# Branch products ahead of the last gate columns, and those gate columns as seven half-size products

## The chip, the cores and the metric

The kernel runs on one core of one Trainium2 chip. The metric is the device time of one execution in microseconds (us). The kernel before takes 646.97 us, the median of 3 runs (646.88 to 647.17). The profiled execution, from which all durations here come, took 647.0 us; its span, from the first to the last instruction of the core, is 645.3 us.

## The reference

One decoder layer on 512 tokens of 1024 channels, all in float32. Only what the change touches is shown in full; the rest is told by its names.

```python
proj = x @ W_in                 # 1024 -> 512 q | 512 k | 512 v | 512 pool_in | 2048 gate logits
y_attn = moba_attention(q, k, v, rel_bias) @ w_branch_attn     # 8 heads x 64, then 512 -> 1024
y_pool = multiscale_pool(p, w_group, scale) @ w_branch_pool    # windows 2, 4, 8, 16, then 512 -> 1024
gates = sigmoid(g).reshape(B, S, 2, 1024)
mixed = gates[:, :, 0] * y_attn + gates[:, :, 1] * y_pool
h = layer_norm(ALPHA * x + mixed @ w_out)
a, u = split(h @ w_ffn_in, 2)                                  # 1024 -> 2 x 2816
a = causal_dwconv(a, conv_w, conv_b)
h = layer_norm(ALPHA * h + (gelu(a) * u) @ w_ffn_out)          # 2816 -> 1024
```

The 2048 gate columns are 16 tiles of 128 columns. Tile f (0 to 7) of the first half gates channels 128 f to 128 f + 127 of the attention branch, tile 8 + f the same channels of the pool branch. The two together are called gate pair f.

## The kernel before

**Numbers.** Every float32 operand is kept as two float32r tiles, `hi` (a rounded copy) and `lo` (the rest). The helper `split` makes them: a copy on ScalarE (line 69) and a subtraction on VectorE (line 70). The helper `mm3` (lines 190 to 192) makes one product as three matmuls: hi times hi, hi times lo, lo times hi. All matmuls take a 128 x 128 tile of weights as the stationary operand, and 512 tokens (or 256) as the moving one.

**Weights.** All weight tiles of the kernel stand in one list, `chunks`, in the order of use. `fetch` loads the next one from memory by the SP queue (line 117) into one of 3 raw buffers and splits it into one of 5 pairs of buffers (`RING`). `weights(i)` fetches up to 3 chunks (`LEAD`) ahead of the one that is used.

**Stages.** In order of the program:
1. The input projection and the attention. `order` lists the 28 tiles of the projection: q, k and pool inputs first, then the 16 gate tiles. Each, `in_tile`, is 8 x 3 matmuls of 512 tokens. `bg` puts the first tiles between the steps of the attention as work for TensorE; the last 9 tiles, all gates, come after the attention. Gate logits are copied to the 12 slots of `gates`; the last four tiles (`NLATE`) go through the sigmoid into `late`.
2. The split of the two branch inputs: `zT` (pool) and `oT` (attention), 4 tiles each.
3. Eight branch tiles, f = 0 to 7. Each is 4 x 3 matmuls of 512 tokens for the pool branch and as many for the attention branch. VectorE multiplies each result with its gate (line 485), GpSimd adds the two (line 488), and the sum is split into `mx_hi`, `mx_lo`. Both lie where `xT_hi` and `xT_lo` lay before.
4. The output projection (`wo`), the residual and the first LayerNorm. GpSimd's queue loads the residual `xs` (line 496) and the LayerNorm rows `lnb` (lines 500, 501) into the place that `gates` held.
5. The channel mixer. Its 22 pairs of columns (a and u) of 128 are computed, for pairs 4 to 17 (`SEVEN`), with seven products in place of eight.
6. The down projection, also with seven products, and the second LayerNorm.

**Seven products.** In `seven(f)` (line 697) a pair is a 2 x 2 block product: the 1024 input channels are cut in two halves, the two column tiles are the two blocks of the output's channels, and the 512 tokens are cut in two. A full pair would be 8 block products; a scheme with sums and differences of blocks needs 7, each of 4 x 3 matmuls of 256 tokens. The sums of weights are formed by loading: the raw tile X is loaded by SP (line 140) and another block is added to it by an accumulating load of GpSimd's queue (line 141); Y is formed from X and A on VectorE (line 152). So a pair has four chunks, A, X, D and Y. The differences of the activations are formed once by `t_form` (line 669) on VectorE, and split: nT1, T3, nT2, T4. Partial results are copied out of PSUM by ScalarE (lines 703, 708, 710) and added by VectorE (lines 712, 714, 715). The last product of a pair waits in `pending` and is issued inside the next pair.

**What sets the order.** A planner orders the instructions of each engine by a simulated timeline; the order in the program is the priority. Work that is ready can so be placed far ahead of its place in the program. The functions:

Of the kernel before, what the change touches and what calls it, by code (L numbers as in the profile page):

```python
# [36 lines left out]
NLATE = 4  # L37
KH = NF // 2
TAIL = 8
SEVEN = tuple(range(4, 18))  # L40
# [5 lines left out]
def layer_kernel(ctx: ExitStack, tc: tile.TileContext, xT, x, w_v, w_c, rel_bias, invcnt, w_group,  # L46
# [27 lines left out]
    spare = [("p", 2), ("p", 3)] + [("g", 8 * g + f) for f in range(KT) for g in range(2)]  # L74
# [8 lines left out]
    BR0 = len(chunks)  # L83
    chunks += [w_br[f] for f in range(KT)]
# [3 lines left out]
    fi_at = {}  # L88
    for f in range(NF):
        for q in "AXDY" if f in SEVEN else "au":  # L90
            fi_at[f, q] = len(chunks)
            chunks.append((f, q) if f in SEVEN else w_fi[2 * f + "au".index(q)])
# [5 lines left out]
    def fetch(pool=None, early=None):  # L98
        i = state["next"]
        state["next"] = i + 1  # L100
        for q, ahead in AHEAD.items():
            while coming[q] and (xu or q == "A") and fi_at[coming[q][0], q] <= i + (ahead if xu else 0):
                fetch_raw(coming[q].pop(0), q)
# [21 lines left out]
    coming = {q: list(SEVEN) for q in "DAX"}  # L125
    xu = None

    def fetch_raw(f, q):
        a, u = w_fi[2 * f], w_fi[2 * f + 1]
        if q == "A":  # L130
            r = wp.tile([P, D], F32, tag="wraw", name=f"araw{f}", bufs=3)
            nc.sync.dma_start(r, a)
        elif q == "D":
            r = xu.tile([P, S], F32, tag="draw", name=f"draw{f}", bufs=2)
            nc.sync.dma_start(r, u[:, S:])
        else:
            r = xu.tile([P, D], F32, tag="xraw", name=f"xraw{f}", bufs=2)
# [6 lines left out]
        raws[f, q] = r  # L144

    def fetch_seven(i, f, q):
        n = S if q == "D" else D
        raw = raws[f, "A" if q == "Y" else q]
        if q == "Y":

            for c, o in ((slice(0, S), raws[f, "X"][:, S:]), (slice(S, D), raw[:, :S])):
                nc.vector.tensor_tensor(raw[:, c], o, raw[:, c], op=ALU.add)
# [35 lines left out]
    def mm3(out_, w, a, start, stop, **kw):  # L188
        (wh, wl), (ah, al) = w, a
        nc.tensor.matmul(out_, wh, ah, start=start, stop=False, **kw)  # L190
# [3 lines left out]
    def split3(v, a):  # L194
        return tuple(t.rearrange("p (a c) -> p a c", a=a) for t in v)

# [150 lines left out]
    def in_tile(n):  # L347
# [11 lines left out]
        elif len(gslot) < NKEEP:  # L359
            gslot[j] = gates[:, len(gslot), :]  # L360
            nc.vector.tensor_copy(gslot[j], b)
        else:
            gslot[j] = late[:, len(gslot) - NKEEP, :]
            nc.scalar.activation(gslot[j], b, AF.Sigmoid)
# [66 lines left out]
    def bg(n=1):  # L431
        for _ in range(n):
            if len(todo) > NLATE:
# [23 lines left out]
    late = bp.tile([P, NLATE, S], F32, name="late")  # L457
# [6 lines left out]
    for k in range(4):  # L464
        split(oT_hi[:, k, :], oT_lo[:, k, :], oT[:, k, :])
    while todo:
        in_tile(todo.pop(0))
    mx_hi = act.tile([P, KT, S], F32R, tag="actT_hi", name="mx_hi")
    mx_lo = act.tile([P, KT, S], F32R, tag="actT_lo", name="mx_lo")
    ext = actp.enter_context(tc.tile_pool(name="ext", bufs=1, side="right"))  # L470
    for f in range(KT):
        if f == KT - LEAD:
            state["limit"] = WO0 + RING - 1
        wh, wl = split3(weights(BR0 + f), KT)
        for g in range(2):
            if gslot[8 * g + f].tensor is gates.tensor:
                nc.scalar.activation(gslot[8 * g + f], gslot[8 * g + f], AF.Sigmoid)
        m = []
        for br in (1, 0):
            b = bank(f"br{f}_{br}")  # L480
            for k in range(4):
                src = (zT_hi[:, k, :], zT_lo[:, k, :]) if br else (oT_hi[:, k, :], oT_lo[:, k, :])
                mm3(b, (wh[:, 4 * br + k, :], wl[:, 4 * br + k, :]), src, k == 0, k == 3)
            t = bp.tile([P, S], F32, tag="m", name=f"m{f}_{br}", bufs=4)
            nc.vector.tensor_tensor(t, gslot[8 * br + f], b, op=ALU.mult)
            m.append(t)
# [198 lines left out]
    for n in ("nT1", "T3", "nT2", "T4"):  # L685
        t_form(n)
# [250 lines left out]
```

## Time and profile before

| what | value |
|---|---|
| median of 3 runs | 646.97 us |
| profiled execution: time, span | 647.0 us, 645.3 us |
| TensorE busy (PE) | 634.8 us, 98% of the span |
| weight loads (PEld) | 551.2 us, 85% |
| VectorE (DVE) | 449.4 us, 70% |
| ScalarE (ACT) | 328.7 us, 51% |
| GpSimd (POOL) | 110.9 us, 17% |
| granted TensorE clock, mean | 0.997 |

The profile page gives the busy time of each engine, the span in 40 slices, the chain of work that ended last, and groups of instructions by line. A row of the timeline reads: start in us, duration in us, engine, line of the kernel, operation, output and inputs by the program's names with their shapes, count, and in brackets how long the engine was idle before and what ended that. Matmuls are pipelined, so the step from one matmul's start to the next is their cost, not the duration of the row. A row of the table by stretches reads: the stretch, its length, then for PE, PEld, DVE, ACT and POOL the busy us (and the count), the granted clock, the busy share of the DMA engines, and GB/s.

### The profile page before, as it was taken

To read this page: it belongs to the slowest core of one execution; us is meant where nothing else is said; L and a number is where in the kernel's file an instruction comes from. 1 tells how busy PE (TensorE), PEld (TensorE's weight loads), DVE (VectorE), ACT (ScalarE), POOL (GpSimd) and SP (SyncE) were. 2 spreads that over 40 slices of the span, in tenths; PEclk is the share of its full clock that TensorE was granted. 3 is DMA by queue.
4 is the path that set the end of the run, shared out by engine and by line. 5 is a ranking of instruction groups with operands and counts; after the bars stand their busy time and mean duration, and the time that the engine had idled before them with its cause. 6 is when DMAs were issued, how large, how long until landed. Compare 5 with 4: busy or idle time off the path is not lost.

```text
span 645.3 us, 9324 instructions
## 1 busy us (share of the span) xinstructions
PE 634.8 (98%) x3586; PEld 551.2 (85%) x3586; DVE 449.4 (70%) x666; ACT 328.7 (51%) x475; POOL 110.9 (17%) x153
## 2 busy tenths in 40 slices
PE   8999999999999999999999999999999999999994
PEld 6888787878788888888998999999998888888884
DVE  6456665564632476489686789888889649698696
ACT  6546556675522233206464555656557337455452
POOL 1605270311000123300010101011101101123202
PEclk9999999999999999999999999999999999999998
DMA  9643222213223236504067576877827964989905
GB/s 318 214 143 113 80 83 82 67 66 99 67 98 99 98 99 245 179 0 137 28 208 168 164 180 163 192 197 184 180 81 276 274 186 102 208 191 194 279 5 130
DMA packets 32540, 94.79 MB, mean 147 GB/s; under 512 B 3688, under 2 KB 3944, under 8 KB 32240
## 3 DMA queue, kind: packets, MB, share of 16 engines
q1 hardware_dynamic: 22832, 66.91, 31.1%
q0 software_dynamic: 9088, 26.24, 20.7%
q10 hardware_dynamic: 576, 1.05, 0.4%
q8 instruction: 28, 0.46, 0.3%
q14 instruction: 16, 0.13, 0.1%
HBM read 91.02 MB, written 3.17 MB: 146 GB/s over the span
## 4 chain that ended last, share of the span: by engine, by line
PE 94%; DVE 2%; POOL 2%; ACT 1%; DMA 0%; issue 0%; DVEq 0%; ACTq 0%; POOLq 0%
PE fi L190 5%; PE fi L192 5%; PE fi L191 5%; PE g L190 5%; PE g L191 5%; PE g L192 5%; PE sa L190 4%; PE sa L192 4%; PE sa L191 4%; PE v L291 3%; PE wo L192 2%; PE br L192 2%; PE br L190 2%; PE wo L190 2%; PE wo L191 2%; PE br L191 2%
## 5 line engine op out<-in xcount | busy, mean ns | idle before, releaser
L70 DVE TENSOR_TENSOR wlo<-wraw,whi 128x1024 fp32r<-128x1024 f32 (+1 forms) x77 | 100.4, 1308 | 50.8 <-ACT whi L69 49.8
L69 ACT ACTIVATE whi<-wraw 128x1024 fp32r<-128x1024 f32 (+1 forms) x76 | 78.8, 1040 | 97.9 <-PE g L191 23.6
L191 PE MATMUL fi<-hT_lo,whi 128*128 128x512 f32 (+1 forms) x168 | 56.7, 339 | 0.0
L192 PE MATMUL fi<-hT_hi,wlo 128*128 128x512 f32 (+1 forms) x168 | 56.7, 339 | 0.0
L190 PE MATMUL fi<-hT_hi,whi 128*128 128x512 f32 (+1 forms) x168 | 56.4, 340 | 0.0
L190 PE MATMUL g<-xT_hi,whi 128*128 128x512 f32 x128 | 50.3, 393 | 0.0
L192 PE MATMUL g<-xT_hi,wlo 128*128 128x512 f32 x128 | 49.9, 390 | 0.0
L191 PE MATMUL g<-xT_lo,whi 128*128 128x512 f32 x128 | 49.8, 389 | 0.0
L141 POOL DMA_DIRECT2D xraw<-in_w_fi x14 | 17.0, 1211 | 180.8 <-DVE y L631 69.0
L69 ACT ACTIVATE whi<-tw 128x1024 fp32r<-128x1024 f32 (+1 forms) x30 | 29.4, 984 | 25.1 <-PE fi L191 12.4
L70 DVE TENSOR_TENSOR wlo<-tw,whi 128x1024 fp32r<-128x1024 f32 (+1 forms) x30 | 33.3, 1126 | 9.3 <-ACT whi L69 9.2
L70 DVE TENSOR_TENSOR wlo<-araw,whi 128x1024 fp32r<-128x1024 f32 x28 | 33.9, 1221 | 6.0 <-ACT whi L69 5.7
L69 ACT ACTIVATE whi<-araw 128x1024 fp32r<-128x1024 f32 x28 | 29.4, 1061 | 13.3 <-PE sa L191 6.1
L192 PEld LDWEIGHTS fi<-hT_hi,wlo 128*128 128x128 f32 x168 | 31.9, 190 | 3.5
L191 PEld LDWEIGHTS fi<-hT_lo,whi 128*128 128x128 f32 x168 | 31.9, 190 | 3.4
L190 PEld LDWEIGHTS fi<-hT_hi,whi 128*128 128x128 f32 x168 | 31.6, 190 | 3.4
L191 PE MATMUL sa<-hT_lo,whi 128*128 128x256 f32 x112 | 31.6, 282 | 0.0
L190 PE MATMUL sa<-hT_hi,whi 128*128 128x256 f32 x112 | 31.6, 282 | 0.0
L192 PE MATMUL sa<-hT_hi,wlo 128*128 128x256 f32 x112 | 31.5, 282 | 0.0
L190 PE MATMUL sb<-T_hi,whi 128*128 128x256 f32 x112 | 31.3, 280 | 0.0
L190 PE MATMUL sa<-nT_hi,whi 128*128 128x256 f32 x112 | 31.3, 279 | 0.0
L192 PE MATMUL sa<-nT_hi,wlo 128*128 128x256 f32 x112 | 31.3, 279 | 0.0
(254 smaller groups left out, 1844.7 us busy)
## 6 DMA issues: line engine op xcount, KB each, us to landing
wraw<-in_w_c SPq DMA_DIRECT2D x28, 512.0 KB, 3.4
tw<-in_w_fo POOLq DMA_DIRECT2D x20, 512.0 KB, 8.3
wraw<-in_w_fi SPq DMA_DIRECT2D x16, 512.0 KB, 3.8
araw<-in_w_fi SPq DMA_DIRECT2D x14, 512.0 KB, 4.6
xraw<-in_w_fi SPq DMA_DIRECT2D x14, 512.0 KB, 4.3
xraw<-in_w_fi POOLq DMA_DIRECT2D x14, 512.0 KB, 6.6
tw<-in_w_fo SPq DMA_DIRECT2D x10, 512.0 KB, 5.8
wraw<-in_w_fo SPq DMA_DIRECT2D x10, 512.0 KB, 6.7
```

The source lines that it names most:

```text
L69: nc.scalar.activation(hi, src, AF.Copy)
L70: nc.vector.tensor_tensor(lo, src, hi.bitcast(F32), op=ALU.subtract)
L141: nc.gpsimd.dma_start(v, bass.AP(tensor=a.tensor, offset=a.offset, ap=[[pst, pn], [u.offset + S - a.offset, 2], [est, S]]), accum_op=ALU.add)
L190: nc.tensor.matmul(out_, wh, ah, start=start, stop=False, **kw)
L191: nc.tensor.matmul(out_, wh, al, start=False, stop=False, **kw)
L192: nc.tensor.matmul(out_, wl, ah, start=False, stop=stop, **kw)
L291: nc.tensor.matmul(bs[j], xs_[j][a], (wh, wl)[b], start=kt == 0 and n == 0, stop=False)
```

## The change

Gate pairs 0 to 3 are computed as before. Gate pairs 4 to 7 become seven products each (`GSEVEN` = 4), with the same scheme and the same functions as the channel mixer. The order becomes: attention with the first 19 projection tiles, one more gate tile, branch tiles 0 to 6, gate pairs 4 to 7 with branch tile 7 around the last products of pair 7, then the output projection.

- `seven`, `s_mm` and `t_form` move to the front and take their operands as arguments. `fetch_raw` takes the place of the raw tiles X and D from a table `homes`.
- The blocks of x that the differences are formed from are loaded again from memory, by four loads on GpSimd's queue, into `qraw`. The four differences are formed in place, one at each of branch tiles 1 to 4; after that, `qraw` serves as the place for X, D and a partial result of the gate pairs.
- Branch results 4 to 6 are copied from PSUM by ScalarE, into free slots of `gates`, until their gates are there.
- The splits of `mx` come after the last gate product, since `mx` lies where `xT` lay.
- Three products at the end are pinned to their place in the program's order.

```diff
-NLATE = 4
+GSEVEN = 4
-    spare = [("p", 2), ("p", 3)] + [("g", 8 * g + f) for f in range(KT) for g in range(2)]
+    spare = [("p", 2), ("p", 3)] + [("g", 8 * g + f) for f in range(GSEVEN) for g in range(2)]
...
-    chunks += [w_br[f] for f in range(KT)]
+    for f in range(KT - 1):
+        add(("br", f), w_br[f])
+    for f in range(GSEVEN, KT):
+        add_seven(("g", f), w_c[first["g"] + f], w_c[first["g"] + KT + f])
+    add(("br", KT - 1), w_br[KT - 1])
...
+    def seven(key, whole, tt, y, u, done, between=None):
+        ba, bb, bc = (bank(f"s{q}{key[0]}{key[1]}") for q in "abc")
+        chain, low, c11 = ba[:, 256:], bb[:, :256], bc[:, :256]
...
+        s_mm(key, "A", 0, b_(k1, t1), chain, True)
+        nc.scalar.activation(y, chain, AF.Copy)
+        s_mm(key, "A", 1, b_(k2, t1), c11, True)
+        flush()
+        s_mm(key, "X", 0, tt["T3"], low, True)
+        nc.scalar.activation(u[:, t2], low, AF.Copy)
+        s_mm(key, "Y", 0, tt["nT2"], chain, False)
+        nc.scalar.activation(u[:, t1], chain, AF.Copy)
+        s_mm(key, "D", 0, tt["T4"], low, False)
+        nc.vector.tensor_tensor(u[:, t1], u[:, t1], low, op=ALU.add)
+        if between:
+            between()
+        s_mm(key, "X", 1, tt["nT1"], chain, False, between)
+        nc.vector.tensor_tensor(u[:, t2], u[:, t2], chain, op=ALU.add)
+        nc.vector.tensor_tensor(ba[:, t1], y, c11, op=ALU.add)
+
+        def close():
+            s_mm(key, "Y", 1, b_(k2, t2), chain, False, between)
+            done(ba, u)
+
+        pending.append(close)
...
+    for n, (k, t) in enumerate(((k1, t1), (k1, t2), (k2, t1), (k2, t2))):
+        nc.gpsimd.dma_start(quads[n], xT[k.start * P:k.stop * P, t].rearrange("(k p) t -> p k t", p=P))
+    state["limit"] = WO0 - 1
     while todo:
         in_tile(todo.pop(0))
...
+    for f in range(KT - 1):
+        if f < GSEVEN:
+            for g in range(2):
+                nc.scalar.activation(gslot[8 * g + f], gslot[8 * g + f], AF.Sigmoid)
+        for br in (1, 0):
+            b = br_mm(f, br)
+            if f < GSEVEN:
+                t = gslot[8 * br + f]
+                nc.vector.tensor_tensor(t, t, b, op=ALU.mult)
+            else:
+                t = branch[f, br] = unused.pop(0)
+                nc.scalar.activation(t, b, AF.Copy)
+        if f < GSEVEN:
+            merged(f, gslot[f], gslot[8 + f])
+            unused.append(gslot[8 + f])
+        if f and forms:
+            t_form(forms[0], tg, *quads)
+            forms.pop(0)
+            if not forms:
+                homes["g", "X"] = lambda f: qraw[1 + 2 * (f % 2)]
+                homes["g", "D"] = lambda f: qraw[2][:, f % 2 * S:(f % 2 + 1) * S]
+
+    def gate_done(f, ba, u):
+        if f < KT - 1:
+            for br, v, scale in ((0, ba, 1.0), (1, u, -1.0)):
+                nc.scalar.activation(v, v, AF.Sigmoid, scale=scale)
+                nc.vector.tensor_tensor(branch[f, br], branch[f, br], v, op=ALU.mult)
+            merged(f, branch[f, 0], branch[f, 1])
...
+    for f in range(GSEVEN, KT):
+        if f == KT - 1:
+            state["limit"] = WO0 + RING - 1
+        own = slice(f % 2 * 256, f % 2 * 256 + 256)
+        seven(("g", f), (xT_hi, xT_lo), tg, zT[:, 0, own], qraw[0][:, f % 2 * S:(f % 2 + 1) * S],
+              lambda ba, u, f=f: gate_done(f, ba, u), first_half if f == KT - 1 else None)
+    bz = br_mm(f, 1, last_bank[0], range(2, 4), True)
+    flush()
+    gxs.close()
...
+    for k in range(KT - 1):
+        split(mx_hi[:, k, :], mx_lo[:, k, :], mts[k])
+    for br, b in ((1, bz), (0, br_mm(f, 0, pin=True))):
+        nc.vector.tensor_tensor(gslot[8 * br + f], gslot[8 * br + f], b, op=ALU.mult)
+    merged(f, gslot[f], gslot[8 + f])
+    split(mx_hi[:, f, :], mx_lo[:, f, :], mts[f])
```

More of the change, by code (lines that the diff above doesn't have):

```diff
@@ L468, in layer_kernel @@
+    flush()
+    gxs.close()
+    ext = actp.enter_context(tc.tile_pool(name="ext", bufs=1, side="right"))
     mx_hi = act.tile([P, KT, S], F32R, tag="actT_hi", name="mx_hi")
     mx_lo = act.tile([P, KT, S], F32R, tag="actT_lo", name="mx_lo")
[L470 to L486, printed above, removed]
-        mt = bp.tile([P, S], F32, tag="mt", name=f"mt{f}", bufs=2)
-        nc.gpsimd.tensor_tensor(mt, m[1], m[0], op=ALU.add)
-        split(mx_hi[:, f, :], mx_lo[:, f, :], mt)
@@ L622, in fi_mm @@
     def fi_mm(j, b, t):
-        wh, wl = split3(weights(fi_at[j // 2, "au"[j % 2]]), KT)
+        wh, wl = split3(weights(at["f", j // 2, "au"[j % 2]]), KT)
         for kt in range(KT):
```

164 lines of the change are left out of this document (93 added, 71 removed).

## The prediction

> **What bounds the kernel now.** I read the page's busy times, the clock and the chain first, then the table by stretches, then the starts of matmuls in the timeline.
>
> ```profile
> span 645.3 us, 9324 instructions
> PE 634.8 (98%) x3586; PEld 551.2 (85%) x3586; DVE 449.4 (70%) x666; ACT 328.7 (51%) x475; POOL 110.9 (17%) x153
> PEclk9999999999999999999999999999999999999998
> PE 94%; DVE 2%; POOL 2%; ACT 1%; DMA 0%; issue 0%; DVEq 0%; ACTq 0%; POOLq 0%
> ```
>
> TensorE (PE) is busy for 98% of the span, is 94% of the chain, and has its full clock. What changes the time is thus the number of matmul steps and any hole between them. The stretches at the change (gate tiles behind the attention, branch tiles) and the stretch of the channel mixer that uses seven products:
>
> ```profile
> 164.25:213.20 48.95, 48.95 (x218) 40.56 (x217) 17.98 (x21) 17.44 (x25) 0.00 (x0) 1.00 0.31 97
> 213.20:256.86 43.66, 43.66 (x195) 36.15 (x194) 28.30 (x28) 13.32 (x16) 11.60 (x12) 1.00 0.39 138
> 349.01:486.90 137.89, 137.89 (x1166) 137.89 (x1165) 116.96 (x161) 82.22 (x123) 14.45 (x12) 1.00 0.66 166
> ```
>
> PE has no idle time in any of them (second and third number of a row). So the change gains only what PE issues less, and loses whatever holes it makes.
>
> **Term 1: gate pairs as seven products.** The price of a pair before: first gate tile after the attention, first branch matmul, first output matmul.
>
> ```profile
> 164.25 0.50 PE L190 MATMUL g<-xT_hi,whi 128*128 128x512 f32 x1
> 213.34 0.39 PE L190 MATMUL br<-zT_hi,whi 128*128 128x512 f32 x1
> 256.86 0.39 PE L190 MATMUL wo<-whi,mx_hi 128*128 128x512 f32 x1
> ```
>
> Nine gate tiles take 49.09 us, 5.45 each; eight branch tiles of the same 24 matmuls take 43.52 us, 5.44 each, or 0.227 us a matmul. A pair is 48 matmuls: 10.88 us. Only one of these nine tiles stays behind the attention as it is; the other eight are the four pairs.
>
> The price after, from the channel mixer: starts of the first products of one pair, and the copy made once a pair (line 703; the first and the last of five such rows, so four pairs lie between).
>
> ```profile
> 349.01 0.28 PE L190 MATMUL sa<-hT_hi,whi 128*128 128x256 f32 x1
> 350.44 0.28 PE L190 MATMUL sc<-hT_hi,whi 128*128 128x256 f32 x1
> 351.88 0.28 PE L190 MATMUL sb<-T_hi,whi 128*128 128x256 f32 x1
> 353.30 0.28 PE L190 MATMUL sa<-nT_hi,whi 128*128 128x256 f32 x1
> ...
> 427.45 0.38 ACT L703 ACTIVATE p1f<-sa 128x256 f32<-128x256 f32 x1 [0.56 <-PE sa L192]
> ...
> 467.11 0.39 ACT L703 ACTIVATE p1f<-sa 128x256 f32<-128x256 f32 x1 [0.56 <-PE sa L192]
> ```
>
> A product of 12 matmuls takes 1.43 to 1.44 us on whole activations and 1.42 on a difference: 3 x 1.44 + 4 x 1.42 = 10.00 us a pair. The copies give (467.11 - 427.45) / 4 = 9.92. I take 9.95, with 9.92 and 10.00 as its ends. One pair saves 10.88 - 9.95 = 0.93 us, four save **3.72 us** (3.5 to 3.8). That is less than the eighth that the scheme removes (1.36 a pair), since a matmul of 256 tokens takes 0.118 us, not half of 0.227.
>
> Here a rule bears on the sum. The Trainium skill, "TensorE: Matmul & The Clock Gate", section "Back-to-back issue gap", puts the step of a warm matmul at N / 2.4 + 2.5 ns, which would be 109 and 216 ns for 256 and 512 columns. By it a pair would go from 10.36 to 9.17 us and the four would save 4.8 us, an estimate from that page. The same section says that in a stream the step is set by weight load and matmul together; the trace agrees with this one, as PEld is busy for all of 137.89 us in the mixer's stretch, against 40.56 of 48.95 in the gate stretch, and the step there is 118 ns. I take the rows.
>
> **Term 2: the branch tiles move up.** Branch tile 0 now follows one gate tile, 5.44 us, after 164.25. Its inputs:
>
> ```profile
> 165.58 2.50 DVE L70 TENSOR_TENSOR zT_lo<-zT,zT_hi 128x512 fp32r<-128x512 f32 x4 [1.45 <-ACT zT_hi L69]
> 168.00 2.49 DVE L70 TENSOR_TENSOR oT_lo<-oT,oT_hi 128x512 fp32r<-128x512 f32 x4
> ```
>
> The pool half is ready at 168.1 and needed at 169.7; the attention half is ready at 170.5 and needed 2.72 us later, at 172.4. Both fit by 1.6 to 1.9 us, so I cost it at nothing; without that cover the price is the delay itself. Their weights keep the lead of three chunks. PE's work in them is the same.
>
> **Term 3: the differences of x, and more vector work.** Four loads on POOL's queue, which had nothing to do there (POOL is 0.00 in the first stretch above), four differences and four splits:
>
> ```profile
> 317.14 2.56 DVE L673 TENSOR_TENSOR hraw<-hraw 128x1024 f32<-128x1024 f32 x2
> 318.40 1.06 ACT L69 ACTIVATE nT_hi<-hraw 128x1024 fp32r<-128x1024 f32 x1 [0.69 <-DVE hraw L673]
> 319.61 1.22 DVE L70 TENSOR_TENSOR nT_lo<-hraw,nT_hi 128x1024 fp32r<-128x1024 f32 x1
> ```
>
> On VectorE that is 4 x (1.28 + 1.22) = 10.0 us, on ScalarE 4.2. The branch stretch has 28.30 us of VectorE work in 43.66, and 5 us of it (eight `mx` splits of 0.6) move to the end, so 33 of 44: it fits, and a delay would hit PE only after 8 PSUM banks of 2.72 us each are full. In the pairs themselves the mixer runs with VectorE at 116.96 of 137.89 us without a hole; a gate pair has fewer operations (two multiplications in place of a convolution). New loads per pair: A, X, D on SP and one accumulation on POOL, the mixer's set, at 166 GB/s there. Hidden; 0.
>
> **Term 4: the start of the first pair.** X and D of pair 4 are loaded into the place of the blocks of x. What that start took in the mixer, from the end of the last difference to Y's split:
>
> ```profile
> 328.22 1.22 DVE L70 TENSOR_TENSOR T_lo<-hraw,T_hi 128x1024 fp32r<-128x1024 f32 x1
> 329.59 0.90 SPq L140 DMA_DIRECT2D xraw<-in_w_fi  x2
> 334.57 1.29 POOL L141 DMA_DIRECT2D xraw<-in_w_fi  x1 [69.03 <-DVE y L631]
> 342.23 0.69 DVE L152 TENSOR_TENSOR araw<-xraw,araw 128x512 f32<-128x512 f32 x1 [3.14 <-DMA xraw<-in_w_fi]
> 345.30 1.22 DVE L70 TENSOR_TENSOR wlo<-araw,whi 128x1024 fp32r<-128x1024 f32 x1
> ...
> 106.20 0.63 ACT L477 ACTIVATE gates<-gates 128x512 f32<-128x512 f32 x1
> ```
>
> 329.4 to 346.5 is 17.1 us; Y is used 4.3 us after the pair's start (349.01 to 353.30). So the differences must end 12.8 us before pair 4 starts at 164.25 + 8 x 5.44 = 207.8, that is by 195.0. If the planner takes them as early as their loads allow, they end near 190: loads from 164.5, some 10 us of issue (twice line 141's 1.29 us, for twice the pieces, an estimate), some 6 to landing, and 10 us of VectorE work shared with the branch tiles. The last row shows that it does take ready work early: this sigmoid is written at the head of the branch tiles and ran 107 us before them. I take 0; the other end is rival D.
>
> **Term 5: the end.** `mx` can be split only when the last gate product has read `xT`. Behind that product PE has 12 pinned matmuls, 2.72 us. In the way of `wo`'s first matmuls:
>
> ```profile
> 350.64 0.38 ACT L703 ACTIVATE p1f<-sa 128x256 f32<-128x256 f32 x1 [0.60 <-PE sa L192]
> 257.17 0.62 ACT L69 ACTIVATE mx_hi<-mt 128x512 fp32r<-128x512 f32 x1
> 259.22 0.68 DVE L70 TENSOR_TENSOR mx_lo<-mt,mx_hi 128x512 fp32r<-128x512 f32 x1
> ```
>
> 0.20 from the next product's start to ScalarE (350.44 to 350.64), two sigmoids of 0.63, 0.62 and 0.68: 2.76 us. The hole is 0.1 us if both sigmoids go ahead, 0 if none does, 2.3 more if a split of weights (1.06 and 1.22) does too. I take 0.1, as the sigmoids come first in the program. Later k need one split each per 2.72 us.
>
> The residual and LayerNorm loads now wait for the last split, since `gates` is in use until then; before, they were issued ahead of `wo`:
>
> ```profile
> 248.24 2.14 POOL L496 DMA_DIRECT2D xs<-in_x  x4
> 262.76 2.79 POOL L501 TENSOR_SCALAR lnb<-lnb 128x1024 f32<-128x1024 f32 x1
> 263.48 0.86 DVE L70 TENSOR_TENSOR mx_lo<-mt,mx_hi 128x512 fp32r<-128x512 f32 x1 [1.85 <-ACT mx_hi L69]
> 282.05 1.40 DVE L539 SCALAR_TENSOR_TENSOR xs<-xs,mv,lnb 128x512 f32<-128x512 f32 x2
> 287.07 1.42 DVE L543 SCALAR_TENSOR_TENSOR xs<-xs,rstd,lnb 128x512 f32<-128x512 f32 x2
> 289.50 1.91 PE L588 MATMUL ht<-ident,xs 128*128 128x128 f32 x16
> DMA to landing us min/median/max: 6.3/9.4/10.0
> ```
>
> With `wo`'s start (256.86) as zero: last split done at 7.5 (263.48 + 0.86), loads issued by 10.2, `lnb` landed at 19.6 (9.4, the last row, for `lnb`), scaled at 22.4. It is needed at 25.2 (282.05), and LayerNorm then ends 1.0 ahead of the transposes. Slack 2.8 + 1.0 us; 0.
>
> **Sum.** Against the profiled execution's 647.0 us, which is the median within 0.05: 647.0 - 3.72 + 0.1 = **643.4 us**, 0.55% faster. Bounds of the terms: 643.2 to 645.9.
>
> **Rivals.**
> - B, the step halves. In the mixer some products on differences do run at half a 512-step:
>
> ```profile
> 473.07 0.28 PE L190 MATMUL sb<-T_hi,whi 128*128 128x256 f32 x1
> 474.44 0.28 PE L190 MATMUL sa<-nT_hi,whi 128*128 128x256 f32 x1
> ```
>
>   1.37 us here. With all seven so, a pair is 9.6 us, and the result 647.0 - 5.1 = 641.9 us; the Trainium skill's formula above gives nearly that (4.8 saved, 642.2). Against it: most products in the mixer take 1.42 or 1.44.
> - C, a hole at the end or at the start of pair 4, of 0.5 to 2.3 us (Term 5's upper end; or X of pair 4 issued only at its place in the program, branch tile 5, two tiles or 10.88 us ahead: 12.8 - 10.88 = 1.9 us). 643.9 to 645.7 us.
> - D, the other side: the last difference runs only at its place, behind branch tile 4, and X, D and A queue on SP behind it. Two branch tiles (10.88 us) less the difference's own 1.28 + 1.06 + 1.22 leave 7.3 us of the 12.8 needed: a hole of 5.5 us, 648.8 us, slower by 0.3%. It decides once the last difference ends after 195.0 plus the gain of 3.7, near 199. For it: the loads of x are late by nature. Against it: the sigmoid at 106.20, and X of pair 4 needs only the second difference gone.
> - E, the change gains nothing: `xs` and `lnb` come 2.5 to 5 us later than the slack of 3.8 allows, PE waits at the transposes, and the gain is given back: 646 to 648 us. For it: `lnb`'s issue moves from before `wo` to 10 us into it. Against: the slack.
>
> **How the numbers follow.** A: 0.60 (643.4). B: 0.08. C: 0.15. D: 0.09. E: 0.08. A measurement of this kernel tells about 0.2% (1.3 us) from no change, so faster means below 645.7. Faster: A, B, C and a little of E, 0.84; same: most of E and a part of D, 0.07; slower: 0.09. The range runs from B's 641.9 to C's end with the upper bound of the terms, 645.9; what is left out is D and E.
>
> **What would show it.** Right: four pairs of 9.9 to 10.0 us between the seventh branch tile and `wo`, no idle PE there, PEld at 100% in that stretch, differences done by 195, `wo`'s start 3.6 us earlier than 256.86, and all later stages earlier by the same. Wrong: PE waiting on X or Y of pair 4, on `mx_lo`, or on the transposes; a pair over 10.3 us.

## The result and the profile after

The changed kernel takes 644.44 us (median of 6 runs, 643.17 to 645.41), beside 646.92 us of the kernel before (median of 6, 646.26 to 647.57): ratio 0.9959, with 0.9945 to 0.9973 as its 95% interval. On a second chip the same kernel took 642.99 us beside 646.43 (ratio 0.9955, 0.9938 to 0.9971). It is faster by 0.4%; the forecast was 643.4 us, 0.55%, in a range from 641.9 to 645.9. Its profiled execution took 644.98 us, with a span of 643.3.

The busy times and the clock, from the page of the changed kernel:

```profile
span 643.3 us, 9708 instructions
PE 631.4 (98%) x3730; PEld 555.0 (86%) x3730; DVE 472.4 (73%) x698; ACT 346.4 (54%) x505; POOL 119.8 (19%) x161
PEclk9999999999999999999999999999999999999998
```

TensorE is still what bounds the kernel, at full clock: 3.4 us less busy, with 23 us more on VectorE and 18 more on ScalarE beside it. Where the stages begin, from the timeline (first gate tile behind the attention, first branch tile, first product of pair 4, first output product):

```profile
163.57 0.50 PE L211 MATMUL g<-xT_hi,whi 128*128 128x512 f32 x1
169.14 0.39 PE L211 MATMUL br<-zT_hi,whi 128*128 128x512 f32 x1
207.22 0.28 PE L211 MATMUL sag<-xT_hi,whi 128*128 128x256 f32 x1
252.96 0.39 PE L211 MATMUL wo<-whi,mx_hi 128*128 128x512 f32 x1
```

From the end of the attention to `wo` it is 252.96 - 163.57 = 89.39 us, where before it was 256.86 - 164.25 = 92.61: the change is worth 3.22 us in its own stages. The other 0.68 of the 3.9 us by which `wo` starts earlier is an earlier end of the attention. That end is not put down to the change: in two other traces of the changed program (below; one of them with each block of x loaded twice) it lies at 162.95 and 164.15, and with another queue for two stores the kernel before has it at 163.16. The table by stretches (length, then busy us of PE, PEld, DVE, ACT, POOL; clock; DMA share; GB/s) for branch tiles 0 to 6, the four pairs with branch tile 7, the output projection, the transposes, and the channel mixer with its plain tiles:

```profile
169.14:207.22 38.08, 38.08 (x169) 31.54 (x168) 28.22 (x28) 14.30 (x17) 11.58 (x7) 1.00 0.58 153
207.22:252.96 45.74, 45.74 (x361) 44.72 (x360) 33.76 (x43) 26.69 (x41) 5.10 (x4) 1.00 0.38 115
252.96:285.61 32.65, 32.65 (x146) 26.98 (x144) 22.36 (x43) 8.87 (x13) 7.20 (x7) 1.00 0.49 178
285.61:298.25 12.64, 12.64 (x65) 10.76 (x64) 11.83 (x23) 8.64 (x14) 0.00 (x0) 1.00 0.32 106
298.25:527.86 229.61, 229.61 (x1698) 219.24 (x1697) 183.86 (x246) 124.28 (x176) 22.14 (x20) 1.00 0.65 178
```

PE is idle in none of them. The stages behind the change are as long as before; the output projection and the mixer of the kernel before:

```profile
256.86:289.50 32.64, 32.64 (x145) 26.99 (x144) 20.11 (x40) 6.27 (x9) 4.90 (x2) 1.00 0.31 105
302.14:531.75 229.61, 229.61 (x1698) 219.24 (x1696) 183.44 (x245) 124.57 (x176) 22.18 (x20) 1.00 0.67 179
```

So the lead of 3.9 us holds up to the down projection, which starts at 527.86 (531.75 before). Then it shrinks: the last matmul starts at 633.87 (636.83 before, 3.0 earlier) and the span is only 2.0 us shorter.

Of the 1.9 us that are lost at the end, 0.9 is a hole of TensorE in the down projection, in a stage that the change does not edit. From the timeline of that stage (the LayerNorm rows for the end, their store, the weights issued behind it, and the matmul that waited):

```profile
586.48 0.56 POOL L635 DMA_DIRECT2D lnb<-in_lnr  x1 [1.58 <-DVE sd_lo L70]
596.70 0.87 SPq L935 DMA_DIRECT2D out<-lnb  x2
597.66 4.69 SPq L193 DMA_DIRECT2D wraw<-in_w_fo  x3
...
608.19 1.06 ACT L69 ACTIVATE whi<-wraw 128x1024 fp32r<-128x1024 f32 x1 [7.63 <-DMA wraw<-in_w_fo]
615.01 0.50 PE L214 MATMUL fod<-wlo,sd_hi 128*128 128x512 f32 x1 [0.64 <-DVE wlo L70]
```

`lnb` landed 10.2 us after its issue; the store on SP waited for it, and three loads of weights stood behind the store on the same queue. The first was split 10.5 us after its issue, and TensorE, whose last matmul ahead had started at 613.99, came to the next at 615.01, 1.02 us later in place of 0.23. The other 0.9 us or so is the last store: the last VectorE instruction ends 4.3 us before the span's end, 3.3 us before.

### The profile page after: what moved, and what is told of

Its sections match the earlier page's. It is cut to its first block, busy times and chain, and to the rows that moved or that the text cites. A ratio compares the mean times of both kernels' runs of the same rounds, so it can differ in the third digit from the quotient of the medians.

```text
span 643.3 us, 9708 instructions
## 1 busy us (share of the span) xinstructions
PE 631.4 (98%) x3730; PEld 555.0 (86%) x3730; DVE 472.4 (73%) x698; ACT 346.4 (54%) x505; POOL 119.8 (19%) x161
## 4 chain that ended last, share of the span: by engine, by line
PE 89%; DMA 4%; DVE 3%; POOL 2%; ACT 1%; issue 1%; SPq 0%; DVEq 0%; ACTq 0%; POOLq 0%
PE fi L214 5%; PE fi L215 5%; PE fi L211 5%; PE saf L211 4%; PE saf L215 4%; PE saf L214 4%; PE v L367 3%; PE g L211 2%; PE g L215 2%; PE g L214 2%; PE br L214 2%; PE br L215 2%; PE wo L214 2%; PE br L211 2%; PE wo L211 2%; PE wo L215 2%
## 5 line engine op out<-in xcount | busy, mean ns | idle before, releaser
L70 DVE TENSOR_TENSOR wlo<-wraw,whi 128x1024 fp32r<-128x1024 f32 (+1 forms) x69 | 84.4, 1228 | 33.3 <-ACT whi L69 32.9
L214 PE MATMUL saf<-hT_lo,whi 128*128 128x256 f32 x112 | 31.6, 282 | 0.0
L211 PE MATMUL saf<-hT_hi,whi 128*128 128x256 f32 x112 | 31.6, 282 | 0.0
L215 PE MATMUL saf<-hT_hi,wlo 128*128 128x256 f32 x112 | 31.5, 282 | 0.0
L211 PE MATMUL sbf<-T_hi,whi 128*128 128x256 f32 x112 | 31.3, 280 | 0.0
L211 PE MATMUL saf<-nT_hi,whi 128*128 128x256 f32 x112 | 31.3, 279 | 0.0
L215 PE MATMUL saf<-nT_hi,wlo 128*128 128x256 f32 x112 | 31.3, 279 | 0.0
L215 PE MATMUL sbf<-T_hi,wlo 128*128 128x256 f32 x112 | 31.2, 279 | 0.0
L214 PE MATMUL saf<-nT_lo,whi 128*128 128x256 f32 x112 | 31.2, 279 | 0.0
L214 PE MATMUL sbf<-T_lo,whi 128*128 128x256 f32 x112 | 31.2, 279 | 0.0
```

Of the source, the lines that this page charges most:

```text
L70: nc.vector.tensor_tensor(lo, src, hi.bitcast(F32), op=ALU.subtract)
L211: ins = nc.tensor.matmul(out_, wh, ah, start=start, stop=False, **kw)
L214: nc.tensor.matmul(out_, wh, al, start=False, stop=False, **kw)
L215: nc.tensor.matmul(out_, wl, ah, start=False, stop=stop, **kw)
```

## The experiments

The first four ran on one chip beside 21 runs of the kernel before (median 646.43 us, 645.8 to 648.49), the next four beside 20 (646.47, 645.81 to 648.84), the last two pairs beside 23 and 11 (646.91, 645.8 to 649.89, and 646.78, 646.03 to 648.22). Ratios are to the kernel before in the same set.

**The new order alone.** Pairs 4 to 7 stay two full tiles each, at the new place; the blocks of x, their differences and the loads for them are left out.

```diff
-        add_seven(("g", f), w_c[first["g"] + f], w_c[first["g"] + KT + f])
+        add(("g", f, "a"), w_c[first["g"] + f])
+        add(("g", f, "u"), w_c[first["g"] + KT + f])
...
-            t_form(forms[0], tg, *quads)
...
-        seven(("g", f), (xT_hi, xT_lo), tg, ...)
+        ba = g_mm(f, "a")
+        gate_done(f, ba, g_mm(f, "u", f == KT - 1))
```

> The order of the change (branch tiles 0 to 6 first, gate pairs 4 to 7 behind them, branch tile 7 at the end, mx splits last), but pairs 4 to 7 as two full tiles of 24 matmuls each, without the blocks of x, without differences, without seven products. My theory (TensorE is bound by the steps it issues, and the move costs and gains nothing): the time of the kernel before, 646.9 us within 0.5; a pair takes 10.88 us; output projection starts as long after the first branch tile as the steps say, without a hole. Rival (the move itself brings part of the 2.5 us, for instance since the splits of mx leave the branch tiles): 645.5 us or less. Rival (the move costs, and seven products hide it): 648 us or more.

Measured: 648.22 us (647.58 to 649.4, 9 runs), ratio 1.0025 (1.0012 to 1.0038). From the end of the attention (163.37) to `wo` (255.98) it is 92.61 us, the same as before to the last digit. So moving the branch tiles costs nothing and gains nothing there, and the whole 3.22 us of the change come from the seven products. The time itself missed the expected 646.9 us and lies where the expectation put the rival, 648 or more: the new order does cost, but behind `wo`. The loss is in the LayerNorm stage (timeline of this kernel):

```profile
303.38 0.68 DVE L638 SCALAR_TENSOR_TENSOR xs<-xs,wo 128x512 f32<-128x512 f32 x1
...
304.64 1.40 DVE L662 SCALAR_TENSOR_TENSOR xs<-xs,rstd,lnb 128x512 f32<-128x512 f32 x2
305.43 0.66 PE L707 MATMUL ht<-ident,xs 128*128 128x128 f32 x4 [0.77 <-DVE xs L662]
```

PE waits 0.77 us for the rescale of the third token tile, which the planner put behind the residual of the fourth (303.38), and the steps around the wait are longer too: from the first transpose to the down projection it is 243.89 us here, 242.25 before, so 1.64 us are lost. In the changed kernel the same rescale runs at 298.38, and PE does not wait for it.

**The changed kernel again, and the two stores on another queue.** The second edit moves the two stores `out<-lnb`, behind which the weights stood in the profile after, from SP's queue to GpSimd's; once in the changed kernel, once in the kernel before.

```diff
-        nc.sync.dma_start(out[i * P:(i + 1) * P, :], lnb[:, 1, :])
+        nc.gpsimd.dma_start(out[i * P:(i + 1) * P, :], lnb[:, 1, :])
```

> The changed kernel, unaltered, for a second trace. In the first one the lead over the kernel before was 3.9 us from the output projection to the middle of the down projection, and 2.0 us at the end: TensorE waited 1.0 us for weights of the down projection that SP had issued behind the stores of the LayerNorm rows, and the last store ended 1.0 us later. Theory 1 (both are chance of memory traffic, in a stage that the change does not touch): executions between 643.0 and 645.5 us, and in this trace the wait is another one, between 0 and 1.5 us. Theory 2 (the change brings them about, by its earlier start of that stage): the same wait of 1.0 us at the same place, and the time at 644.4.

> The changed kernel with the two stores of the LayerNorm row (out from lnb, in the down projection) issued by GpSimd's queue behind its own scaling, in place of SP's. SP then does not wait for the row, and its loads of the last weights go out earlier. Theory 1 (the lost 1 us is this wait): no idle TensorE in the down projection, and 643.0 to 643.6 us, in a narrower spread. Rival (the loads are late since the memory traffic is full there, not since SP waits): the wait stays, 644 to 645 us.

> The kernel before with the same two stores on GpSimd's queue. Its trace shows no wait of TensorE there. Theory 1: 646.3 to 647.0 us, so that the change is worth 3.2 to 3.7 us between the two kernels with this edit. Rival (the wait is in most executions of before as well, and the trace happens not to show it): 645.5 us or less.

Measured: the changed kernel again 642.99 us (642.73 to 646.08, 7 runs); with the stores moved 643.33 (643.02 to 644.06, 5 runs), ratio 0.9952 (0.9937 to 0.9966); the kernel before with the stores moved 646.48, ratio 1.0 (0.9991 to 1.0009). The hole at `fod` is in neither trace of the first two: it comes and goes with the same program. From issue to landing, the three loads of weights that stand behind the store took, in the changed kernel, in its second trace and with the stores moved:

```profile
DMA to landing us min/median/max: 9.1/10.4/11.8
```
```profile
DMA to landing us min/median/max: 8.8/9.0/11.0
```
```profile
DMA to landing us min/median/max: 5.6/5.8/8.2
```

The weights land sooner with the stores moved, but the median time is no lower. So the wait behind the store is real, and that moving it makes the kernel faster is not shown. The kernel before has the same wait (its three loads took 8.8, 11.0 and 9.1 us) and no hole. What goes with the hole is when the first of the three lands. Two of the kernels below, with x and h moved and with the half way offset, have the hole as well. In these two traces and the first of the changed kernel that load landed 80.2 to 80.4 us behind the start of the down projection; in the nine others with the store on SP, the kernel before among them, it landed after 77.2 to 79.0, and there is no hole. In all three traces of the changed order, attention to `wo` is 89.39 us.

**Three pairs, and five pairs.** `GSEVEN` = 5 and 3 (with five pairs, one slot of `gates` more is handed on).

```diff
-GSEVEN = 4
+GSEVEN = 5
```

> Three gate pairs (5 to 7) as seven products in place of four. If the gain is the pair's price alone, 10.88 less 10.06, the stretch from the end of the attention to the output projection grows from 89.39 to 90.2 us and the time is 0.8 us above the changed kernel. If a fixed cost or gain of the new order hides in the 3.2 us, the stretch moves by more or less than 0.8.

```diff
-GSEVEN = 4
+GSEVEN = 3
...
             merged(f, branch[f, 0], branch[f, 1])
+            unused.append(branch[f, 1])
```

> Five gate pairs (3 to 7) as seven products. The pair saves another 0.8 us (10.88 less 10.06). But only 18 projection tiles are then left to run within the attention in place of 20, so that TensorE has nothing to put into two of its steps: if the attention needs them, holes of 1 to 5 us come up there and the time is 0 to 4 us above the changed kernel; if the planner fills the gaps from elsewhere, it is 0.8 us below.

Measured, three pairs: 644.55 us (643.76 to 646.91, 10 runs), ratio 0.9968 (0.9955 to 0.9981). Attention to `wo` is 253.28 - 163.07 = 90.21 us, 0.82 more than with four, as expected: a pair is worth 0.82 us, and four of them make 3.28 us beside the 3.22 measured, so no fixed cost or gain above 0.1 us hides behind it.

Five pairs: 647.34 us (646.65 to 649.75, 10 runs), ratio 1.0015 (1.0003 to 1.0027). Two rows of its timeline and two of its table by stretches (attention's second half up to the first branch tile, and the five pairs with branch tile 7):

```profile
162.32 0.50 PE L211 MATMUL br<-zT_hi,whi 128*128 128x512 f32 x1 [1.20 <-ACT zT_hi L69]
163.05 0.50 PE L214 MATMUL br<-zT_lo,whi 128*128 128x512 f32 x1 [0.23 <-DVE zT_lo L70]
```
```profile
97.09:162.32 65.23, 63.14 (x317) 48.86 (x315) 34.86 (x76) 43.41 (x76) 13.71 (x21) 1.00 0.32 102
201.06:256.86 55.80, 55.80 (x445) 54.79 (x444) 42.51 (x55) 32.58 (x50) 8.78 (x7) 1.00 0.55 152
```

The fifth pair costs 55.80 - 45.74 = 10.06 us, like the others. But `wo` starts at 256.86, 3.9 us later than with four: two plain gate tiles are gone. One of them had filled steps of the attention, which now has 6 gate tiles in place of 7; the other had stood between the attention and the first branch tile, which now follows at once and waits for the split of `zT` (the two rows above). PE is idle for 2.1 us in the first of these stretches, where the changed kernel has no idle time up to 163.57. The cover of Term 2 is gone.

**The differences later.** Each block of x is loaded twice into its place; what is computed is the same.

```diff
-        nc.gpsimd.dma_start(quads[n], xT[...])
+        for _ in range(2):
+            nc.gpsimd.dma_start(quads[n], xT[...])
```

> Each of the four blocks of x is loaded twice into the same place, the second time with the same values, so that the differences start later by the second load's issue and landing; the computation is the same. The forecast gave the differences until 195.0 us, and in the changed kernel the last split ended at 188.4, so 6.6 us are free: if the loads finish less than that later, no hole before pair 4 and the time is the changed kernel's within 0.5 us. By the rule of rival D (the price counts from 195.0 on) a last split at 198 gives a hole of 3 us at the start of pair 4, and 646 us.

Measured: 644.17 us (643.52 to 644.93, 5 runs), ratio 0.9963 (0.9949 to 0.9977). The last split of the differences, the first of Y for pair 4, and the stretch of the pairs in this kernel:

```profile
194.07 1.21 DVE L70 TENSOR_TENSOR gT_lo<-quad,gT_hi 128x1024 fp32r<-128x1024 f32 x1
...
203.63 1.23 DVE L70 TENSOR_TENSOR wlo<-araw,whi 128x1024 fp32r<-128x1024 f32 x1 [0.85 <-ACT whi L69]
```
```profile
207.81:253.54 45.73, 45.73 (x361) 44.73 (x360) 33.75 (x43) 26.68 (x41) 6.29 (x5) 1.00 0.43 123
```

The last split ends at 195.28, 7 us later than in the changed kernel, and PE still has no idle time: attention to `wo` is 89.39 us again. It took 9.6 us from there to Y's split (204.86), not the 17.1 us that the forecast took from the mixer. The run goes past the forecast's deadline of 195.0 by 0.28 us only, so where the hole begins is not measured. The time is 1.2 us above the changed kernel's on another chip, with intervals that overlap; the stages do not show it, except that the attention ends 0.6 us later in this trace.

**Where the operands lie.** In the changed kernel the products of one pair do not cost the same. The first rows of products that follow each other (T3, nT2, whole x, nT1, then whole x), in the changed kernel:

```profile
210.10 0.28 PE L211 MATMUL sbg<-gT_hi,whi 128*128 128x256 f32 x1
211.54 0.28 PE L211 MATMUL sag<-gnT_hi,whi 128*128 128x256 f32 x1
212.98 0.28 PE L211 MATMUL sag<-xT_hi,whi 128*128 128x256 f32 x1
...
215.86 0.28 PE L211 MATMUL sag<-gnT_hi,whi 128*128 128x256 f32 x1
217.27 0.29 PE L211 MATMUL scg<-xT_hi,whi 128*128 128x256 f32 x1
```

T3 and nT2 take 1.44 us each, nT1 takes 1.41, with the same shape. The program gives nT1 an address that is a multiple of 256 bytes; T3, nT2, T4, x and the weights all lie 192 bytes beyond one. Five kernels move these places with unused gaps; what is computed stays the same. (The raw places `quad` between the differences move with them; no matmul reads those.) The first:

```diff
     tg = {"nT1": ...}
-    gx.tile([P, 304], F32, name="gx_gap2")
     qraw = ...
     for n in parts[1:]:
         tg[n] = ...
+    gx.tile([P, 304], F32, name="gx_gap2")
```

> The changed kernel with an unused gap of 1216 bytes per partition moved behind the split differences T3, nT2 and T4, so that these three lie 1216 bytes lower; nothing else differs. In the changed kernel a product on T3, nT2 or T4 takes 1.44 us and one on nT1 takes 1.41 us, with the same shapes and instructions. Theory: the step at 256 tokens depends on where the moving operand lies; with the three blocks at the same offset within 4096 bytes as nT1, their products go to 1.41 us, a pair from 10.06 to 9.97 us, and the stretch from the end of the attention to the output projection from 89.39 to 89.0 us. Rival: the step is set by the weights or by what runs beside it; then the products stay at 1.44 and the stretch at 89.4 us. Either way the time is within 0.5 us of the changed kernel's 643 us.

The second and third, x and h moved too, then the weights (where the weights' gap also moves the tiles behind it, the others are taken out):

```diff
     xT_lo = act.tile(...)
+    act.tile([P, 48], F32, name="act_gap")
...
-    gx.tile([P, 304], F32, name="gx_gap2")
...
+    hTp.tile([P, 16], F32, name="hT_gap")
     hT_hi = hTp.tile(...)
```
```diff
     wp = ...
+    wp.tile([P, 16], F32, name="w_gap")
...
+    act.tile([P, 48], F32, name="act_gap")
...
-    gx.tile([P, 16], F32, name="gx_gap")
...
-    gx.tile([P, 304], F32, name="gx_gap2")
```

> The changed kernel with three unused gaps moved or resized, so that all moving operands of the seven products (x, h and their differences, in both stages) start at a multiple of 256 bytes; in the changed kernel only the mixer's differences and nT1 do, and x, h, T3, nT2 and T4 of the gate pairs start at 192 bytes beyond one. Theory, from the run with the differences moved: the start within 256 bytes sets the step, 120 ns at 192 and 118 ns at 0. Then the three products of a pair on whole x or h go from 1.44 to 1.42 us too, 0.07 us a pair, 1.3 us over 18 pairs, and with the 0.3 of the moved differences the time is about 1.5 us below the changed kernel. If the quick products of 1.36 us (step 113 ns), which now appear in some pairs of the mixer behind products on h, become the rule, up to 8 us. Rival: the 1.44 us of the products on whole x and h come from their stride between channel tiles, not from their start; then they stay and only the 0.3 us show.

> As the run before, and the split weights start at a multiple of 256 bytes too (they start at 192 beyond one in all other kernels). If the place of the stationary operand sets the step, products change from 1.42 us, in either direction; if it does not, the time is that of the run before.

The fourth is the first with h moved too; the fifth sets h and the differences 64 bytes higher still:

```diff
+    hTp.tile([P, 16], F32, name="hT_gap")
```
```diff
-    gx.tile([P, 16], F32, name="gx_gap")
+    gx.tile([P, 32], F32, name="gx_gap")
...
-    gx.tile([P, 304], F32, name="gx_gap2")
...
+    hTp.tile([P, 32], F32, name="hT_gap")
```

> The kernel with the differences moved (T3, nT2 and T4 of the gate pairs at 0 within 256 bytes), and hT 64 bytes higher, at 0 too; x and the weights stay at 192. By the two runs before, a step of 256 tokens takes 120 ns where the moving operand and the weights start at the same offset within 256 bytes and 118 ns where they differ, and a step of 512 tokens 227 and about 230 ns. So x, which is mostly read in steps of 512, is best left at the weights' offset, and hT, mostly read in steps of 256, moved off it. Expected: attention to output projection 89.1 us, first tile of the channel mixer to the down projection 229.0 us in place of 229.6, and 0.9 us less in all than the changed kernel, 642.1 us beside 643.0.

> As the run before, with hT and the four differences of the gate pairs at 64 within 256 bytes, 128 away from the weights' offset in place of 64. If only equal or different counts, the stages and the time are those of the run before; if the distance counts, the steps of 256 tokens move from 118 ns, and the gate pairs from 9.99 us, in either direction.

The three products after the first two of pair 4 with the differences moved (timeline; T3, nT2, whole x):

```profile
209.77 0.28 PE L211 MATMUL sbg<-gT_hi,whi 128*128 128x256 f32 x1
211.19 0.28 PE L211 MATMUL sag<-gnT_hi,whi 128*128 128x256 f32 x1
212.60 0.29 PE L211 MATMUL sag<-xT_hi,whi 128*128 128x256 f32 x1
```

T3 and nT2 now take 1.42 and 1.41. The stretches of the five kernels, in the order above (each one's gate pairs with branch tile 7, then others that changed: the output projection, and the mixer with its plain tiles):

```profile
206.90:252.36 45.46, 45.46 (x361) 44.45 (x360) 33.94 (x43) 26.66 (x41) 5.08 (x4) 1.00 0.37 118
```
```profile
209.21:254.31 45.10, 45.10 (x361) 44.09 (x360) 34.11 (x43) 26.56 (x41) 5.09 (x4) 1.00 0.41 125
254.31:287.63 33.32, 33.32 (x146) 26.98 (x145) 22.84 (x44) 8.89 (x13) 7.18 (x7) 1.00 0.48 175
...
300.48:529.43 228.95, 228.95 (x1697) 218.10 (x1696) 183.80 (x246) 123.30 (x175) 22.14 (x20) 1.00 0.65 177
```
```profile
207.02:252.84 45.82, 45.82 (x362) 44.82 (x360) 33.76 (x43) 26.66 (x41) 5.09 (x4) 1.00 0.40 122
252.84:285.48 32.64, 32.64 (x145) 26.98 (x144) 22.63 (x44) 8.87 (x13) 7.19 (x7) 1.00 0.47 178
298.12:529.66 231.54, 231.54 (x1697) 221.22 (x1696) 184.01 (x246) 123.51 (x176) 22.14 (x20) 1.00 0.64 176
```
```profile
207.08:252.54 45.46, 45.46 (x361) 44.45 (x360) 33.93 (x43) 26.65 (x41) 5.08 (x4) 1.00 0.48 126
...
297.83:526.83 229.00, 229.00 (x1698) 218.11 (x1696) 183.77 (x246) 123.94 (x176) 22.14 (x20) 1.00 0.67 178
```
```profile
206.92:252.46 45.54, 45.54 (x362) 44.51 (x360) 33.92 (x43) 26.66 (x41) 5.09 (x4) 1.00 0.42 125
297.74:528.25 230.51, 230.51 (x1697) 218.77 (x1696) 183.97 (x246) 124.08 (x176) 22.16 (x20) 1.00 0.66 178
```

The same with the bytes beyond a multiple of 256 at which the operands start (d: T3, nT2, T4 of the gate pairs; nT1 is at 0 but in the last row, where it is at 64; w: the weights; the mixer's own differences are at 0 throughout):

| kernel | x, d, h, w | pairs and branch tile 7 | output projection | mixer | time, us | ratio |
|---|---|---|---|---|---|---|
| changed kernel | 192, 192, 192, 192 | 45.74 | 32.65 | 229.61 | 642.99 | 0.9955 (0.9938 to 0.9971) |
| differences moved | 192, 0, 192, 192 | 45.46 | 32.65 | 229.60 | 642.95 | 0.9951 (0.9932 to 0.997) |
| x and h moved too | 0, 0, 0, 192 | 45.10 | 33.32 | 228.95 | 644.88 | 0.9973 (0.9959 to 0.9988) |
| weights moved too | 0, 0, 0, 0 | 45.82 | 32.64 | 231.54 | 645.43 | 0.9979 (0.9965 to 0.9992) |
| differences and h | 192, 0, 0, 192 | 45.46 | 32.65 | 229.00 | 642.95 | 0.994 (0.9928 to 0.9952) |
| half way | 192, 64, 64, 192 | 45.54 | 32.65 | 230.51 | 644.86 | 0.9968 (0.9955 to 0.998) |

(Each ratio is to the kernel before on the same chip; the times come from four chips.)

What sets the step is not the moving operand's start alone but how it stands to that of the weights. With both at 192, or both at 0, the products of the pairs and of the mixer take steps of 120 ns (119.9 to 120.0 in the mean over the steps of the gate pairs with the weights moved too); with the one at 0 and the other at 192 they take 117.8 to 118.0 (117.4 on the mixer's differences in the changed kernel, by a short step named below). Only the place within 256 bytes counts: within 512 bytes x stands 256 off the weights in the changed kernel and h 0, and both take 120 ns. So the rival in the second expectation, the stride of whole x and h, falls: they go to 1.42 us when they are moved. Its theory was right only while the weights stayed at 192: with the weights moved too, all of the gain was gone, and the steps were the longest.

For steps of 512 tokens it is the other way round. With x moved off the weights' offset, a gate tile's step goes from 227.7 to 229.9 ns in the mean and that of a q tile from 227.7 to 231.3, and the output projection grows by 0.67 us (its stationary operand `mx` lies where x did). The pairs and the mixer gain 1.3 us in that kernel, but its first gate tile behind the attention starts late, since all tiles of the projection read x:

```profile
165.48 0.51 PE L211 MATMUL g<-xT_hi,whi 128*128 128x512 f32 x1
```

In the other traces of this document in which a gate tile follows the attention, it starts between 162.95 and 164.25. So the projection and the output projection lose more than the pairs and the mixer gain.

Half way, 128 bytes apart, the steps of whole h scatter from 115 to 122 ns, and those of the mixer's plain tiles with 512 tokens take 232.7 ns in place of 229.0; the mixer with its plain tiles is 1.5 us longer than in the row above, two thirds of it by the latter. The distance counts, not only whether the two differ.

Two of these kernels hold a test inside one stage. With x and h moved, three of the eight weight tiles of the output projection moved to 0 too: the steps on these, where both operands start at 0, take 227.9 ns in the mean, and those on the other five, still at 192, take 233.3. With the weights moved too, one of the two stationary tiles of the down projection stayed at 192: steps on it take 228.9 ns, steps on the other, at 0 like the weights, 226.7; the few steps of 256 columns on the first take 113.6 ns, where they take 119.3 with both at 192. A short step of 113 ns also appears on 88 of the 672 steps on differences in the mixer of the changed kernel, and on none where h is moved to 0; why it is 113 there and 118 elsewhere, at the same two offsets, is not explained.

The kernel with differences and h moved does what its expectation said, stage by stage: 89.11 us from attention to `wo` (252.54 - 163.43), 229.00 in the mixer. Its ratio is the lowest of all (642.95 us, 642.38 to 643.6, beside 646.78); the interval overlaps the changed kernel's, so that it is faster than that one is shown by the stages (0.28 and 0.61 us) and not by the time.

## Why the prediction was right

- **What bounds the kernel.** Right. PE is idle nowhere from the attention to the down projection, and what it issues less is what was gained.
- **Term 1** was mis-sized. The pairs with branch tile 7 take 45.74 us; branch tile 7 has 5.5 of them, so a pair costs 10.06 us, above the forecast's upper end of 10.00, and the four save 3.3 in place of 3.72. The failed step is "4 x 1.42 on a difference": that was the mixer's price, where the differences and the weights do not start at the same offset; here three of the four do, and cost 1.44 like whole x. With the differences moved a pair costs 9.99, the forecast's upper end. The price per pair then holds from three pairs to five.
- **Rival B** did not occur. The Trainium skill, "TensorE: Matmul & The Clock Gate", section "Back-to-back issue gap", gives 109 and 216 ns for its isolated step, and about 131 ns for 512 columns in a stream; the steps measured here are 113 to 122 for 256 columns and, as means, 227 to 233 for 512, so the trace does not agree with either figure for 512.
- **Term 2** was right, by the run with the order alone (92.61 us to 92.61) and by the one with five pairs, which shows the price where the cover is gone.
- **Term 3** was right in its 0 and wrong in a row: the four loads of x were issued at 152.49 and took 3.03 us of GpSimd's queue, not some 10 us from 164.5 on. Their place became free before the attention ended.
- **Term 4** was right: the last split ended at 188.4 (185.11 + 3.28, below), where 190 was forecast and 195.0 was the limit. The limit itself was too strict in its length: with the split at 195.28, Y was ready 9.6 us later. By that, rival D's last difference, 7.3 us ahead of the pair and used 4.3 us behind its start, would have cost less than the 5.5 us given, perhaps nothing; this was not run.
- **Term 5.** `wo` started without a hole (0 for 0.1; the term's own parts give 2.76 - 2.72 = 0.04). The loads were later than forecast, and little slack was left. The LayerNorm loads, their scaling and the first reader in the changed kernel:

```profile
262.89 2.20 POOL L631 DMA_DIRECT2D xs<-in_x  x4 [6.66 <-DVE mx_lo L70]
265.09 0.53 POOL L635 DMA_DIRECT2D lnb<-in_lnr  x1
276.85 2.79 POOL L636 TENSOR_SCALAR lnb<-lnb 128x1024 f32<-128x1024 f32 x1 [11.23 <-DMA lnb<-in_lnr]
...
279.67 1.42 DVE L674 SCALAR_TENSOR_TENSOR xs<-xs,mv,lnb 128x512 f32<-128x512 f32 x2 [0.28 <-POOL lnb L636]
```

  With `wo` as zero, `lnb` was scaled at 26.7, not 22.4: the last split came at 9.6 rather than 7.5, and the load took 11.7 us to land rather than 9.4. VectorE waited 0.28 us for it, the last two rescales ran up to 285.78, and the transposes began at 285.61 without a wait; the last four of this group, which read what the last rescale wrote, began at 286.92. So rival E stayed out by about 1.1 us, not by 3.8. The run with the order alone, with another order of VectorE's work, did wait at the transposes and lost 1.6 us, by a rescale of a later token tile.
- **What was missing** is the end: the forecast had the later stages earlier by the same amount, and of the 3.9 us at `wo` the profiled execution kept 2.0. The hole at `fod` and the longer last store have no term in it. In the second trace of the same program the hole is absent and the stretch behind VectorE's last instruction is 3.5 us, not 4.3 (its span is 641.0 us), and the runs lie from 642.73 to 646.08 us. What makes `lnb` and the weights land later in some executions stays open. That `wo` started 3.9 us earlier, where 3.6 was forecast, is in part luck: its stages gave 3.22, and the other 0.68 is the earlier end of the attention, which is no term of the sum.

The time came out in the range because the mechanism of the gain was right and the errors (0.4 us in Term 1, up to 1.9 us at the end) were smaller than the range.

## What to carry to other kernels

The price of a scheme that runs elsewhere in the same kernel is a good forecast, but take it apart by operand first: here the same product cost 1.41 or 1.44 us by where its operand lay against the weights, and a gap of 64 bytes moved a stage by 0.6 us. When work is moved, look up what its loads waited for: a place freed late (`gates`) uses up slack that the table of stages does not show. A loss of 1 us at the far end can cancel part of a gain of 3, so compare two executions of the same program before it is put down to the change.

## What the runs showed of the hardware

- The step of a matmul depends on how the moving and the stationary operand start within 256 bytes: 120 ns where they start alike against 118 (in one stage 113.6) where one is at 0 and the other at 192, for 256 columns; 227 ns against 229 to 233, the other way round, for 512. The Trainium skill, "SBUF — State Buffer", section "Who interferes with whom", gives TensorE two independent read ports for them and only VectorE and GpSimd a shared one. These runs show that the two reads are not independent in their timing; which part of the chip couples them was not tested.
- VectorE and GpSimd hold each other up. In the changed kernel (timeline):

```profile
177.30 2.20 POOL L564 TENSOR_TENSOR gates<-gates 128x512 f32<-128x512 f32 x1 [21.77 <-DVE gates L577]
178.27 2.31 DVE L70 TENSOR_TENSOR gT_lo<-quad,gT_hi 128x1024 fp32r<-128x1024 f32 x1
...
185.11 3.28 DVE L70 TENSOR_TENSOR gT_lo<-quad,gT_hi 128x1024 fp32r<-128x1024 f32 x1
185.52 1.78 POOL L564 TENSOR_TENSOR gates<-gates 128x512 f32<-128x512 f32 x1
```

  The same subtraction takes 1.21 us where no addition of GpSimd lies beside it (194.07, above), and 2.31 and 3.28 us where one does; both times it ends 1.1 us behind the addition's end. An addition of the same size takes 1.30 us beside the gate pairs (234.74), and 2.20 in the first row, which begins 0.17 us behind the start of another split. The same section of that page says that such a pair locks a shared port for whole instructions; the trace agrees, as the first subtraction is longer by 1.1 us, about the part of GpSimd's 2.20 us that was still to run (1.23). The second does not fit it as well: by the trace it began 0.41 us ahead of the addition, and yet it ended behind it.
